# A hybrid attention, state space and dilated attention block on one core: 64-row attention operands without zeros, other queues for the state space transfers, another order of the first loads

## The chip, the cores and the metric

One core of a Trainium2 chip runs the whole program. The time is the device time of one execution in microseconds (us). The engines of the core are PE (TensorE, matmuls), DVE (VectorE), ACT (ScalarE), POOL (GpSimd) and SP (SyncE, which issues most DMAs). Weights come from HBM through SBUF; matmuls write PSUM, which DVE and ACT empty.

## The reference, cut to what matters

Two layers over 256 tokens of width 1024, in fp32. The first has three branches on one projection: MLA (causal attention of 8 heads with 128 channels of nope and 64 of rope), gated linear attention in chunks (GLA) and attention to a memory of 256 tokens (4 heads of 64 channels), gated and summed, and then a feed-forward net (FFN). The second has a state space branch (S5, here as a chunked convolution and a scan over chunks) and dilated attention (3 groups of 8 heads with 64 channels).

```python
q_full = jnp.concatenate([q_nope, q_pe], axis=-1)          # 128 + 64 channels
k_full = jnp.concatenate([k_nope, jnp.broadcast_to(k_pe, (B, S, MLA_HEADS, MLA_ROPE))], axis=-1)
o_mla = causal_block_attention(q_full, k_full, v_mla, (MLA_NOPE + MLA_ROPE) ** -0.5)
...
s_m = jnp.einsum('bshd,bmhd->bhsm', q_m, k_m).astype(jnp.float32) * (MEM_DQK ** -0.5)   # 64 channels
p_m = jax.nn.softmax(s_m, axis=-1).astype(v_m.dtype)
...
bu_re = jnp.einsum('blgp,gnp->blgn', u_c, bb_re)           # the state space: 64 groups, 16 channels, 64 states
y = jnp.einsum('blgn,gpn->blgp', h_re, cr) - jnp.einsum('blgn,gpn->blgp', h_im, ci)
...
s = jnp.einsum('bqhd,bqjhd->bqhj', q_blk[:, :, g], kg) * scale   # dilated: 64 channels a head
```

## The kernel before

The code doesn't call the engines at once. A recorder (L538) writes every operation into a plan, and `Plan.order` (L356) sets the order in which each engine gets its instructions: `Plan.price` (L283) gives each operation a cost, `latest` (L320) works back from the end to due times, and `order` walks forward through time and takes for each engine the ready operation with the earliest due time. `boost` raises some of them, the first loads above all, by `START` (L163). All is emitted at one line (L535), so the rows of the profile all say L535 and are told apart by their tiles: ps is PSUM, wr a weight chunk as loaded, wh and wl its fp32r main part and remainder (written by ACT and DVE), k tiles of activations (their pools k2, k4 and kx are not told apart), c constants, sm small ones. `nc.any` lets the plan choose DVE or ACT.

The large products are in fp32r, three passes (high by high, high by low, low by high), each of 256 or 512 columns. Attention is in fp32, which the profile shows as two records of MATMUL for each instruction. What the parts of the change touch:

- `apart` (L774) writes a transposed operand with two heads, one on rows 0 to 63 and one on 64 to 127, into two tiles that are zero in the other half (GpSimd writes the zeros). With them the scores of one 64-channel head are a matmul over all 128 rows. It serves MLA's rope keys (`kpT`, L937), the memory keys (`kmT`, L891) and the keys of dilated group 0 (`heads`, L1543).
- `mla_attn` (L1154) does for each head the scores of the nope channels and of the rope channels into one PSUM tile (128 columns for the first 128 queries, 256 for the others), then softmax on DVE and ACT, transposes on PE, and the product with the values. `mem_attn` (L1092) and `dilated` (L1578) are alike; `dilated` adds the 64 by 64 blocks of groups 1 and 2 behind each group 0 product.
- `ssm_quarter` (L1367, four times, recorded among the FFN) makes the S5 matrices: PE transposes them, one copy for each half of them goes from PSUM to `gx`, and four SBUF to SBUF DMAs on SP bring its four quarters to `g`, on other partitions. A Toeplitz table is written to DRAM (`kz`, two DMAs a quarter) and `ssm_toeplitz` (L1436) reads it back in 16 pieces T of 16 partitions. `ssm_in` (L1461) sends u to DRAM (`ud`) and reads it back regrouped as U; all on SP's queue, among the weights.
- `inputs1` (L847) and `weights` (L603) set the start: gains, memT and the first w_mv chunks on SP's queue. The first w_mv chunk comes in two halves.

Of the kernel before, what the change touches and what calls it, by code (L numbers as in the profile page):

```python
# [19 lines left out]
P = 128  # L20
S = 256
# [124 lines left out]
PE, ACT, DVE, POOL, SP = "tensor", "scalar", "vector", "gpsimd", "sync"  # L146
# [8 lines left out]
START = {"w_mv": 0, "x": 7.2, "rows": 16, "mem": 20, "w_mk": 40}  # L155
WARM = 10
NORM = 500000
# [10 lines left out]
LAG.update({(ACT, ACT): 145, (PE, PE): 0, (DVE, PE): 220, (ACT, PE): 240})  # L168
READ_FIRST = ("copy_predicated",)
# [6 lines left out]
class Plan:  # L176
# [379 lines left out]
class Net:  # L556
# [46 lines left out]
    def weights(self, name, idx, nk, n):  # L603
# [3 lines left out]
        for i in range(nk // 2):  # L607
# [5 lines left out]
            for k in [slice(0, 1), slice(1, 2)] if name == "w_mv" and idx + i == 0 else [slice(0, 2)]:  # L613
# [160 lines left out]
    def apart(self, z, gain=None):  # L774


        nc = self.nc
        half = slice(0, 64), slice(64, P)
        for i in range(2):
            nc.gpsimd.memset(z[i][half[1 - i]], 0.0)  # L780

        def evac(b, n, p):
            for i in range(2):
                nc.any.copy(z[i][half[i], b:b + n], p[half[i]], *([] if gain is None else [gain[half[i]]]))
        return evac

# [60 lines left out]
    def inputs1(self):  # L847
# [10 lines left out]
        self.gains = self.load_const("gains", [P, GW])  # L858
# [21 lines left out]
    def mem_kv(self):  # L880
# [10 lines left out]
        self.kmT = [self.t2([P, 2, S]) for _ in range(2)]  # L891
        self.transposed(km.rearrange("p t h d -> p t (h d)"), 2, self.apart(self.kmT, self.g("g_k_mem")))
# [21 lines left out]
    def ckv(self):  # L914
# [22 lines left out]
        self.kpT = [self.const([P, 1, S]) for _ in range(2)]  # L937
        self.transposed(kd.rearrange("p t h d -> p t (h d)"), 1, self.apart(self.kpT))
# [153 lines left out]
    def mem_attn(self):  # L1092
# [7 lines left out]
        for hh in range(4):  # L1100
            p = self.aux([P, 512])
# [3 lines left out]
            pr = self.t2([P, 512])  # L1105
            self.softmax_rows(p, pr, [256, 256])
            pT = self.aux([P, 2, S])
# [259 lines left out]
    def ssm_quarter(self, qd):  # L1367
# [58 lines left out]
        k = 1  # L1426
# [400 lines left out]
```

## Time and profile before

| | us |
|---|---|
| median of 3 runs (lowest to highest) | 864.33 (863.37 to 865.55) |
| the profiled execution, its own time | 864.48 |
| its span, first to last instruction | 862.7 |
| busy in the span: PE, DVE, ACT, POOL | 845.5, 630.5, 471.6, 5.4 |
| mean granted clock of TensorE | 0.997 |

Busy time of an engine is the time in which it has at least one instruction. Matmuls are pipelined, and the shown duration of one holds its latency too, so that what a matmul costs is read from the start of one to the start of the next. "PEclk" is the granted clock, 1.00 for 2.4 GHz. Idle time ahead of a row stands in brackets with the operation that ended it. SPq is SP's DMA queue: the time beside it is that of issuing, not of moving the data.

### The profile page before, as it was taken

Reading aid. Unit: us, or ns where it says so; the run is one execution under the profiler, and the core shown is the slowest. Engines: PE = TensorE matmul, PEld = TensorE weight load, DVE = VectorE, ACT = ScalarE, POOL = GpSimd, SP = SyncE. Lnnn points to the kernel's source line nnn. Section 1 sums busy time; section 2 is a strip of 40 time slices with the busy share of each in tenths; the row PEclk is TensorE's granted clock in tenths of the full one; section 3 lists DMA queues with packets and bytes.
Section 4 is the critical chain, followed back from the end, with each engine's and each line's share of the span. In section 5 each row is a group of like instructions: output and inputs, shape, how many; then the busy total and the mean of one; then the engine's idle time right before and its main releaser. Section 6 shows DMA issues by size and latency. Waiting matters only on the chain.

```text
span 862.7 us, 16680 instructions
## 1 busy us (share of the span) xinstructions
PE 845.5 (98%) x6572; PEld 757.2 (88%) x6572; DVE 630.5 (73%) x1484; ACT 471.6 (55%) x754; POOL 5.4 (1%) x13
## 2 busy tenths in 40 slices
PE   8999998999999999999999999899999999999998
PEld 6988877889999989999999888787789769999996
DVE  6999999995766669964445755969997665653584
ACT  6767756645445557555555564446466653554352
POOL 2000000000000000000000000000000000000000
PEclk9999999999999999999999999999999999999999
DMA  8874433035455564555555579670445404555551
GB/s 317 255 243 150 149 125 119 1 120 177 141 176 175 190 237 154 195 195 193 185 186 182 196 170 237 225 219 29 148 146 174 145 25 138 180 172 195 182 178 56
DMA packets 60750, 144.19 MB, mean 167 GB/s; under 512 B 24560, under 2 KB 25712, under 8 KB 60672
## 3 DMA queue, kind: packets, MB, share of 16 engines
q1 hardware_dynamic: 60672, 143.13, 50.7%
q8 instruction: 51, 0.84, 0.4%
q14 instruction: 27, 0.22, 0.1%
HBM read 138.46 MB, written 2.56 MB: 163 GB/s over the span
## 4 chain that ended last, share of the span: by engine, by line
PE 84%; DVE 9%; DMA 2%; ACT 1%; issue 1%; SPq 1%; DVEq 0%; ACTq 0%
PE ps L535 84%; DVE k L535 6%; DVE wl L535 2%; DVE sm L535 1%; SPq L535 1%; ACT k L535 1%; DMA wr<-w_mv 1%; DMA wr<-w_k 1%; ACT wh L535 0%; DMA k<-k 0%; DVE c L535 0%; DVEq L1815 0%; ACTq L535 0%; DVEq L535 0%
## 5 line engine op out<-in xcount | busy, mean ns | idle before, releaser
L535 DVE TENSOR_TENSOR wl<-wr,wh 128x1024 fp32r<-128x1024 f32 (+2 forms) x257 | 300.8, 1193 | 164.0 <-ACT wh L535 161.5
L535 ACT CAST wh<-wr 128x1024 fp32r<-128x1024 f32 (+2 forms) x257 | 257.6, 1028 | 232.7 <-PE ps L535 214.1
L535 PE MATMUL ps<-k,wh 128*128 128x256 f32 x2048 | 371.3, 283 | 0.3 <-DVE k L535 0.3
L535 PEld LDWEIGHTS ps<-k,wh 128*128 128x128 f32 x2048 | 320.2, 192 | 2.0 <-DVE k L535 0.5
L535 PE MATMUL ps<-wh,k 128*128 128x512 f32 (+2 forms) x1024 | 313.8, 384 | 2.3 <-ACT wh L535 2.2
L535 PE MATMUL ps<-k,wl 128*128 128x256 f32 x1024 | 289.9, 283 | 1.9 <-DVE wl L535 1.9
L535 PEld LDWEIGHTS ps<-wh,k 128*128 128x128 f32 x1024 | 188.8, 188 | 38.7 <-ACT wh L535 3.3
L535 PEld LDWEIGHTS ps<-k,wl 128*128 128x128 f32 x1024 | 196.4, 192 | 3.0 <-DVE wl L535 2.3
L535 PE MATMUL ps<-wl,k 128*128 128x512 f32 (+2 forms) x512 | 196.9, 386 | 1.3 <-DVE wl L535 1.2
L535 PEld LDWEIGHTS ps<-wl,k 128*128 128x128 f32 x512 | 96.2, 188 | 21.0 <-DVE wl L535 3.6
L535 DVE TENSOR_TENSOR k<-k,k 128x512 f32<-128x512 f32 (+8 forms) x192 | 91.8, 497 | 13.2 <-ACT k L535 12.7
L535 PE MATMUL ps<-k,k 64*64 64x64 f32 (+6 forms) x1224 | 83.5, 253 | 2.6 <-ACT k L535 1.4
L535 PEld LDWEIGHTS ps<-k,k 64*64 64x64 f32 (+4 forms) x1224 | 62.4, 139 | 21.3 <-issue 12.3
L535 ACT ACTIVATE k<-ps 128x512 f32<-128x512 f32 (+2 forms) x86 | 44.4, 531 | 45.9 <-PE ps L535 45.7
L535 ACT COPY k<-ps 128x512 f32<-128x512 f32 (+7 forms) x98 | 44.1, 491 | 35.0 <-PE ps L535 31.5
L535 ACT ACTIVATE k<-k 128x512 f32<-128x512 f32 (+3 forms) x71 | 45.9, 673 | 24.3 <-DVE k L535 23.4
L535 PE MATMUL ps<-c,k 128*128 128x128 f32 (+1 forms) x344 | 54.3, 286 | 4.2 <-DVE k L535 3.0
L535 PEld LDWEIGHTS ps<-c,k 128*128 128x128 f32 x344 | 41.2, 147 | 11.8 <-DVE k L535 3.9
L535 DVE TENSOR_TENSOR k<-k,c 128x64 f32<-128x64 f32 (+7 forms) x176 | 47.6, 314 | 0.0
L535 ACT ACTIVATE k<-ps,c 128x256 f32<-128x256 f32 (+3 forms) x79 | 38.5, 544 | 14.0 <-PE ps L535 12.0
L535 DVE SCALAR_TENSOR_TENSOR k<-k,k 128x256 fp32r<-128x256 f32 (+4 forms) x61 | 32.6, 567 | 12.3 <-ACT k L535 12.1
L535 ACT ACTIVATE k<-k,sm 128x384 f32<-128x384 f32 (+2 forms) x32 | 16.8, 528 | 10.9 <-DVE sm L535 10.9
(73 smaller groups left out, 302.7 us busy)
## 6 DMA issues: line engine op xcount, KB each, us to landing
wr<-w_up SPq DMA_DIRECT2D x32, 512.0 KB, 3.6
wr<-w_down SPq DMA_DIRECT2D x32, 512.0 KB, 3.6
wr<-w_gt SPq DMA_DIRECT2D x24, 512.0 KB, 4.1
wr<-w_o SPq DMA_DIRECT2D x16, 512.0 KB, 3.8
wr<-w_k SPq DMA_DIRECT2D x12, 512.0 KB, 4.1
wr<-w_q SPq DMA_DIRECT2D x12, 512.0 KB, 4.2
wr<-w_v SPq DMA_DIRECT2D x12, 512.0 KB, 3.3
wr<-w_qkg SPq DMA_DIRECT2D x8, 512.0 KB, 4.3
```

The costliest lines, as they stand in the source:

```text
L535: getattr(getattr(tc.nc, op.eng), op.name)(*map(live, op.args), **{k: live(v) for k, v in op.kw.items()})
```

## The change

- `apart` is gone. Keys with 64 channels stay in one tile, two heads on its two row halves, and the scores of a head are a matmul of 64 rows by 128 columns on its half. In `mla_attn` both heads of a pair get their PSUM tile first; the code writes the nope products of both, and then the rope products in turns between the halves. `mem_attn` goes by pairs too, in turns. `dilated` changes its operands only.
- `price` halves the cost of such a matmul, and a GpSimd DMA is 700 there instead of 1000.
- `gx` and its four DMAs a quarter are gone: eight half-size copies a quarter go from PSUM straight to the right partitions of `g`, where two stood before.
- kz, T, ud and U transfers are issued by GpSimd (`nc.gpsimd`).
- gains is issued by ACT. The first two w_mv chunks come in halves (`HALVES`), and x is due behind more w_mv chunks (12.2 in `START`, 7.2 before).

```diff
-START = {"w_mv": 0, "x": 7.2, "rows": 16, "mem": 20, "w_mk": 40}
+START = {"w_mv": 0, "x": 12.2, "rows": 16, "mem": 20, "w_mk": 40}
+HALVES = 2
...
-            return {SP: 50, ACT: 50, POOL: 1000}[op.eng]
+            return {SP: 50, ACT: 50, POOL: 700}[op.eng]
...
-            if half:
-                return 2 * (2 * n / 2.4 + cols / 1.2 - 8)
-            return 2 * (max(2 * n / 2.4, cols / 1.2) + 9)
+            return (1 if half else 2) * (max(2 * n / 2.4, cols / 1.2) + 9)
...
-            for k in [slice(0, 1), slice(1, 2)] if name == "w_mv" and idx + i == 0 else [slice(0, 2)]:
+            for k in [slice(0, 1), slice(1, 2)] if name == "w_mv" and idx + i < HALVES else [slice(0, 2)]:
...
-        self.gains = self.load_const("gains", [P, GW])
+        self.gains = self.const([P, GW])
+        nc.scalar.dma_start(out=self.gains, in_=I["gains"])
...
-        self.kpT = [self.const([P, 1, S]) for _ in range(2)]
-        self.transposed(kd.rearrange("p t h d -> p t (h d)"), 1, self.apart(self.kpT))
+        self.kpT = self.const([P, 1, S])
+        self.transposed(kd.rearrange("p t h d -> p t (h d)"), 1, lambda b, n, p: nc.any.copy(self.kpT, p))
...
+            ps = [self.aux([P, 512]) for _ in HALF]
             for t in range(2):
-                nc.tensor.matmul(p[:, t * S:(t + 1) * S], qmT[:, hh // 2, t * P:(t + 1) * P],
-                                 self.kmT[hh % 2][:, hh // 2], start=True, stop=True)
+                for i, hs in enumerate(HALF):
+                    nc.tensor.matmul(ps[i][:, t * S:(t + 1) * S], qmT[hs, hp, t * P:(t + 1) * P],
+                                     self.kmT[hs, hp], start=True, stop=True)
...
+            ps = [self.aux([P, 384]) for _ in HALF]
+            for i, p in enumerate(ps):
                 hh = 2 * hp + i
-                kp = self.kpT[i][:, 0]
-                nc.tensor.matmul(p[:, 0:P], qn(0), self.kT[hh][:, 0:P], start=True, stop=False)
-                nc.tensor.matmul(p[:, 0:P], qp(0), kp[:, 0:P], start=False, stop=True)
-                nc.tensor.matmul(p[:, P:384], qn(1), self.kT[hh], start=True, stop=False)
-                nc.tensor.matmul(p[:, P:384], qp(1), kp, start=False, stop=True)
+                nc.tensor.matmul(p[:, 0:P], self.qT[hh][:, 0:P], self.kT[hh][:, 0:P], start=True, stop=False, skip_group_check=True)
+                nc.tensor.matmul(p[:, P:384], self.qT[hh][:, P:], self.kT[hh], start=False, stop=False, skip_group_check=True)
+            for t, ks in enumerate((slice(0, P), slice(P, 384))):
+                for p, hs in zip(ps, HALF):
+                    nc.tensor.matmul(p[:, ks], self.qpT[hs, hp, t * P:(t + 1) * P], self.kpT[hs, 0, 0:P * (t + 1)],
+                                     start=False, stop=True, skip_group_check=True)
...
-        for gh in range(2):
-            for par in range(2):
-                nc.sync.dma_start(out=g[64 * gh:64 * gh + 64, :, par], in_=gx[64 * par:64 * par + 64, :, gh])
+            for gh in range(2):
+                for par in range(2):
+                    nc.any.copy(g[64 * gh:64 * gh + 64, 4 * ri:4 * ri + 4, par], p[64 * par:64 * par + 64, :, 64 * gh:64 * gh + 64])
...
-                    self.nc.sync.dma_start(out=self.T[par][o:o + 16],
+                    self.nc.gpsimd.dma_start(out=self.T[par][o:o + 16],
...
-                nc.sync.dma_start(out=ud[qd].rearrange("(gs q) (e c) -> (q e) gs c", gs=8, e=8),
+                nc.gpsimd.dma_start(out=ud[qd].rearrange("(gs q) (e c) -> (q e) gs c", gs=8, e=8),
...
-                    nc.tensor.matmul(pp[i][:, 0:S], self.q2[0][:, b, tt * P:tt * P + P], self.k2T[0][i][:, b],
+                    nc.tensor.matmul(pp[i][:, 0:S], self.q2[0][a, b, tt * P:tt * P + P], self.k2T[0][a, b],
```

The plan sets a new order for the whole program. First PE, in the MLA attention. Of before, the end of one head (ps_2341) and the next one of the pair (ps_2367): the PSUM tile takes nope products (from k_405) and rope products (c_2 and c_6 are the two zero-padded key tiles, k_399 the rope queries) by turns, all over 128 rows.

```order
L535 MATMUL ps_2341<-c_2_95,k_399_1596 128x256
L535 MATMUL ps_2330<-k_543_2322,k_419_1666 128x128
L535 MATMUL ps_2367<-k_405_1619,k_546_2332 128x128
L535 MATMUL ps_2367<-c_6_105,k_399_1596 128x128
L535 MATMUL ps_2367<-k_405_1619,k_546_2332 128x256
L535 MATMUL ps_2367<-c_6_105,k_399_1596 128x256
```

Of after, the two heads of a pair (ps_2282 and ps_2307): the products from c_383 (rope keys) and k_387 (rope queries) are the 64-row ones, each head's on its own row half.

```order
L535 MATMUL ps_2282<-k_393_1584,k_518_2245 128x128
L535 MATMUL ps_2282<-k_393_1584,k_518_2245 128x256
L535 MATMUL ps_2282<-c_383_1550,k_387_1562 128x128
L535 MATMUL ps_2282<-c_383_1550,k_387_1562 128x256
L535 MATMUL ps_2299<-c_39_232,k_511_2211 128x128 x4
L535 MATMUL ps_2307<-k_393_1584,k_518_2245 128x128
L535 MATMUL ps_2307<-k_393_1584,k_518_2245 128x256
L535 MATMUL ps_2307<-c_383_1550,k_387_1562 128x128
L535 MATMUL ps_2307<-c_383_1550,k_387_1562 128x256
```

The two 64-row products of a head now stand behind its two full-array ones, and between the two heads of the pair stand other full-array matmuls. In the memory attention, after, the same in a closer mix (ps_2448 to ps_2491 are the scores of the four heads, 64 rows each; c_39 is the identity of the transposes):

```order
L535 MATMUL ps_2448<-k_408_1634,k_581_2437 128x256 x2
L535 MATMUL ps_2439<-k_584_2444,k_403_1621 128x256
L535 MATMUL ps_2466<-k_408_1634,k_581_2437 128x256
L535 MATMUL ps_2469<-c_39_232,k_575_2411 128x128
L535 MATMUL ps_2466<-k_408_1634,k_581_2437 128x256
L535 MATMUL ps_2439<-k_584_2444,k_406_1628 128x128
L535 MATMUL ps_2480<-k_408_1634,k_581_2437 128x256
L535 MATMUL ps_2469<-c_39_232,k_575_2411 128x128 x2
L535 MATMUL ps_2480<-k_408_1634,k_581_2437 128x256
L535 MATMUL ps_2491<-k_408_1634,k_581_2437 128x256 x2
```

The heads of ps_2448 and ps_2480 lie on rows 0 to 63, those of ps_2466 and ps_2491 on rows 64 to 127; before, each head's two products stood together, over all rows. Counted over the whole program, PE changes the shape of its tile 120 times before and 156 times after. On DVE, 623 instructions stand ahead of the last of the twelve softmax reciprocals of MLA and memory attention before, and 561 after.

Second the queues of the state space. Before, SP has all of it between the weights (kz writes, the copies to `g` as k<-k, ud, T as k<-kz, U as k<-ud):

```order
L535 DMA k_1308_6434<-k_1295_6342 64x8x64 x4
L535 DMA ud_58<-k_1309_6471 128x8x64
L535 DMA k_1315_6498<-kz 16x16x64 x7
L535 DMA wr_6516<-w_u 128x1024
L535 DMA wr_6524<-w_k 128x1024
L535 DMA k_1315_6498<-kz 16x16x64
L535 DMA k_1319_6535<-kz 16x16x64
L535 DMA k_1320_6539<-ud_58 128x512
L535 DMA k_1319_6535<-kz 16x16x64 x3
L535 DMA wr_6566<-w_k 128x1024
```

After, GpSimd's queue has it, in this order, with nothing else between:

```order
L535 DMA kz<-k_1274_6274 64x2x64 x2
L535 DMA k_1301_6389<-kz 16x16x64 x8
L535 DMA k_1305_6466<-kz 16x16x64 x5
L535 DMA ud_58<-k_1310_6502 128x8x64
L535 DMA k_1305_6466<-kz 16x16x64 x3
L535 DMA k_1314_6546<-ud_58 128x512
L535 DMA ud_59<-k_1310_6502 128x8x64
L535 DMA k_1314_6546<-ud_59 128x512
```

SP keeps only the weights there. On GpSimd sixteen T transfers stand ahead of U's first read, thirteen of them ahead of the write of ud; on SP nine stood ahead of it, all behind that write.

## Rows read from the trace of the kernel before

**Rows 1.** From the page: busy time, share and instructions of each engine, and the chain of work that ended last, its shares by engine.

```profile
PE 845.5 (98%) x6572; PEld 757.2 (88%) x6572; DVE 630.5 (73%) x1484; ACT 471.6 (55%) x754; POOL 5.4 (1%) x13
...
PE 84%; DVE 9%; DMA 2%; ACT 1%; issue 1%; SPq 1%; DVEq 0%; ACTq 0%
```

**Rows 2.** From the timeline of PE around 143 to 151 us (MLA attention): start in us, us to the end of the group, engine, line, operation, output and inputs, rows by columns of the array, shape; x counts records, two for an fp32 matmul.

```profile
143.03 1.82 PE L535 MATMUL ps<-c,k 128*128 128x128 f32 x10 [1.69 <-DVE k L535]
...
148.93 0.38 PE L535 MATMUL ps<-k,k 128*128 128x128 f32 x2
149.99 0.49 PE L535 MATMUL ps<-k,k 128*128 128x128 f32 x2 [0.68 <-ACT k L535]
150.32 0.39 PE L535 MATMUL ps<-c,k 128*128 128x128 f32 x2
150.54 0.60 PE L535 MATMUL ps<-k,k 128*128 128x256 f32 x2
150.97 0.70 PE L535 MATMUL ps<-c,k 128*128 128x256 f32 x3
```

**Rows 3.** From the timeline of PE at the decay gate (the product of 16 rows), columns as in rows 2.

```profile
74.68 0.28 PE L535 MATMUL ps<-k,wl 128*128 128x256 f32 x1
74.80 0.40 PE L535 MATMUL ps<-k,wh 128*128 128x256 f32 x2
75.13 1.12 PE L535 MATMUL ps<-c,k 16*128 16x256 f32 x4
76.19 0.39 PE L535 MATMUL ps<-k,wl 128*128 128x256 f32 x1
76.41 0.27 PE L535 MATMUL ps<-c,k 128*128 128x128 f32 x1
```

**Rows 4.** From the timeline of PE in the dilated attention, columns as in rows 2; the first row holds 15 matmuls of 64 by 64 and two of 128 by 256.

```profile
679.14 2.48 PE L535 MATMUL ps<-k,k 64*64 64x64 f32 x34
681.55 0.50 PE L535 MATMUL ps<-wl,k 128*128 128x512 f32 x1
```

**Rows 5.** From the groups of instructions of PE by line, operation, tile and form over the whole span: records, busy us, mean ns of one, idle before.

```profile
L535 PE MATMUL ps<-k,k 64*64 64x64 f32 x768 | 29.6, 223 | 1.6 <-DMA k<-ud 0.6 <-DVE k L535 0.5 <-ACT k L535 0.4
...
L535 PE MATMUL ps<-k,k 128*64 128x64 f32 x64 | 4.3, 227 | 0.0
```

**Rows 6.** From the windows by stage of the attention region: stretch, its us, busy time (instructions) of PE, PEld, DVE, ACT and POOL, granted clock, DMA share, GB/s.

```profile
126.50:141.00 14.50, 14.50 (x302) 13.07 (x292) 14.11 (x67) 10.35 (x24) 0.00 (x0) 1.00 0.24 78
141.00:150.00 9.00, 6.56 (x63) 5.15 (x52) 7.29 (x21) 4.15 (x11) 0.00 (x0) 0.81 0.62 204
150.00:158.00 8.00, 7.70 (x51) 6.87 (x52) 7.82 (x46) 4.92 (x16) 0.00 (x0) 1.00 0.10 38
166.00:174.00 8.00, 8.00 (x44) 6.73 (x43) 8.00 (x46) 5.33 (x14) 0.00 (x0) 1.00 0.01 3
```

**Rows 7.** From the timeline of SP's DMA queue at the start.

```profile
1.19 0.42 SPq L535 DMA_DIRECT2D c<-gains  x1
1.66 0.42 SPq L535 DMA_DIRECT2D wr<-w_mv  x1
```

**Rows 8.** From the timeline of ACT at the start.

```profile
4.75 0.62 ACT L535 CAST wh<-wr 128x512 fp32r<-128x512 f32 x1 [0.76 <-DMA wr<-w_mv]
...
6.93 0.62 ACT L535 CAST wh<-wr 128x512 fp32r<-128x512 f32 x1 [0.86 <-DMA wr<-w_mv]
8.82 0.91 ACT L535 ACTIVATE k<-k,c 128x256 fp32r<-128x256 f32 x2 [1.28 <-DMA k<-memT]
10.11 1.04 ACT L535 CAST wh<-wr 128x1024 fp32r<-128x1024 f32 x1 [0.37 <-DMA wr<-w_mv]
```

**Rows 9.** From the timeline of SP's DMA queue at the state space transfers, us of issuing and count in each row.

```profile
508.80 5.43 SPq L535 DMA_DIRECT2D k<-k  x8
514.28 1.99 SPq L535 DMA_DIRECT2D kz<-k  x3
...
519.14 0.58 SPq L535 DMA_DIRECT2D ud<-k  x1
519.90 4.65 SPq L535 DMA_DIRECT2D k<-kz  x7
```

**Rows 10.** From the windows of the same stretch, columns as in rows 6.

```profile
500.00:520.00 20.00, 18.93 (x206) 17.70 (x205) 11.08 (x34) 11.64 (x29) 0.00 (x0) 1.00 0.76 168
520.00:545.00 25.00, 22.81 (x171) 19.20 (x170) 14.80 (x23) 10.74 (x13) 0.00 (x0) 1.00 0.93 246
```

**Rows 11.** From the timeline of PE, ACT and DVE from 530 to 546 us (u, and the first products of the state space).

```profile
532.27 0.33 PE L535 MATMUL ps<-k,k 64*64 64x64 f32 x4 [0.64 <-DMA k<-ud]
...
534.88 1.05 ACT L535 CAST wh<-wr 128x1024 fp32r<-128x1024 f32 x1 [3.34 <-DMA wr<-w_k]
...
542.19 1.21 DVE L535 TENSOR_TENSOR_SCAN k<-k,k 128x512 f32<-128x512 f32 x1
...
544.08 1.21 DVE L535 TENSOR_TENSOR wl<-wr,wh 128x1024 fp32r<-128x1024 f32 x1
...
545.34 0.39 PE L535 MATMUL ps<-k,wl 128*128 128x256 f32 x1 [1.89 <-DVE wl L535]
```

**Rows 12.** From the DMA issues by tile: count, KB of each, median us from issue to landing.

```profile
ud<-k SPq DMA_DIRECT2D x4, 256.0 KB, 5.0
...
k<-ud SPq DMA_DIRECT2D x4, 256.0 KB, 4.3
```

More of the change, by code (lines that the diff above doesn't have):

```diff
@@ L168 @@
 LAG.update({(ACT, ACT): 145, (PE, PE): 0, (DVE, PE): 220, (ACT, PE): 240})
+HALF = slice(0, 64), slice(64, P)
 READ_FIRST = ("copy_predicated",)
@@ L772, in split @@
             nc.vector.scalar_tensor_tensor(lo, src, scale, h.bitcast(F32), ALU.mult, ALU.subtract)
[L774 to L785, printed above, removed]
     def row_rms(self, x, n):
@@ L890, in mem_kv @@
         km = self.normed(ps, 0, 4, 64, r)
-        self.kmT = [self.t2([P, 2, S]) for _ in range(2)]
-        self.transposed(km.rearrange("p t h d -> p t (h d)"), 2, self.apart(self.kmT, self.g("g_k_mem")))
+        self.kmT = self.t2([P, 2, S])
+        self.transposed(km.rearrange("p t h d -> p t (h d)"), 2,
+                        lambda b, n, p: nc.any.copy(self.kmT[:, b:b + n], p, self.g("g_k_mem")))
     def norm_x(self):
@@ L1157, in mla_attn @@
             o = self.aux([P, 2, S])
[L1158 removed]
+            ps = [self.aux([P, 384]) for _ in HALF]
+            for i, p in enumerate(ps):
                 hh = 2 * hp + i
[L1160 to L1167 removed]
+                nc.tensor.matmul(p[:, 0:P], self.qT[hh][:, 0:P], self.kT[hh][:, 0:P], start=True, stop=False, skip_group_check=True)
[4 more added lines that the diff above has]
+                                     start=False, stop=True, skip_group_check=True)
+            for i, p in enumerate(ps):
+                hh = 2 * hp + i
                 pr = self.t2([P, 384])
@@ L1349, in ssm_small @@
         nc.vector.memset(z, 0.0)
-        nc.sync.dma_start(out=self.kz.rearrange("g a j q x -> (g a j q) x")[:, 0:48].rearrange("(p r) x -> p r x", r=8), in_=z)
+        nc.gpsimd.dma_start(out=self.kz.rearrange("g a j q x -> (g a j q) x")[:, 0:48].rearrange("(p r) x -> p r x", r=8), in_=z)
         self.G, self.Cx, self.R = [], [], []
@@ L1548, in heads @@
             self.rope(q[:, :, :, 0:16], 8, ta, tb, 8, q[:, :, :, 0:16])
-            if g == 0 and nm == "kr":
-                qt = [self.t4([P, 4, S]) for _ in range(2)]
-                evac = self.apart(qt, self.g(gain, g))
-            else:
-                qt = self.t4([P, 4, S])
-                evac = lambda b, n, p: self.nc.any.copy(qt[:, b:b + n], p, self.g(gain, g))
-            self.transposed(q.rearrange("p t h d -> p t (h d)"), 4, evac)
+            qt = self.t4([P, 4, S])
+            self.transposed(q.rearrange("p t h d -> p t (h d)"), 4,
+                            lambda b, n, p: self.nc.any.copy(qt[:, b:b + n], p, self.g(gain, g)))
             dst.append(qt)
@@ L1589, in dilated @@
                 pp = [self.aux([P, 384]) for _ in half]
-                for i in range(2):
-                    nc.tensor.matmul(pp[i][:, 0:S], self.q2[0][:, b, tt * P:tt * P + P], self.k2T[0][i][:, b],
+                for i, a in enumerate(half):
+                    nc.tensor.matmul(pp[i][:, 0:S], self.q2[0][a, b, tt * P:tt * P + P], self.k2T[0][a, b],
                                      start=True, stop=False, skip_group_check=True)
```

41 lines of the change are left out of this document (18 added, 23 removed).

## The prediction

> **What bounds the kernel now.** I read the page first. TensorE (PE) is busy for 98% of the span and the chain that ended last is 84% PE, with 9% DVE [rows 1]. So the time is the sum of PE's issue times, plus the places where PE waits for someone, and an edit counts only if it shortens the first or takes away one of the second. The reader should therefore look for two things in the rest: what a 64-row matmul costs on PE, and where PE stands still.
>
> For the first I read PE's timeline at two places and the groups of PE by form. At 150 us the full-array fp32 matmul (two records, one for each pass) takes 0.22 us for 128 columns of output and 0.43 us for 256, from start to start [rows 2]. The kernel before has one matmul that uses few rows and all 128 columns, the 16-row one of the decay gate: two of them take 1.06 us (75.13 to 76.19) between fp32r matmuls [rows 3]. That is 0.53 each, not less than the full array's 0.43. The fp32r matmul behind them starts its successor after 0.22 us, where its neighbours take 0.12, and the two ahead take 0.33 in place of 0.24. So the excursion into another tile shape and back costs (1.06 - 0.86) + 0.10 + 0.09 = 0.39 us, about 0.195 for each of two switches, and fewer rows by themselves buy nothing. A second place bounds it from below: 15 matmuls of 64 by 64 and two of 128 by 256 lie between 679.14 and 681.55 [rows 4]. By 0.058 each (they alternate between row halves; the whole group's busy time gives 29.6/384 = 0.077, [rows 5]) and 0.43 each they would need 0.87 + 0.86 = 1.73 of the 2.41 us, which leaves 0.68 for five switches, 0.14 each.
>
> For the second I read the windows by stage. From 126 to 184 us DVE is nearly always busy; between 141 and 150 PE is busy for only 6.56 of 9 us and its granted clock is 0.81 [rows 6]; the half-speed level (1.2 GHz) lies right behind PE's longest idle stretch there, 1.69 us ahead of 143.03, which ended with DVE [rows 2].
>
> **The change part by part.**
>
> *Unpadded halves.* Forty matmuls (16 of the MLA rope scores, 8 of the memory attention, 16 of the dilated group 0) lose their 64 rows of zeros. By rows 3 each keeps its length when it stands alone. It would be cheaper if two of them ran side by side on the two row halves: the 64 by 64 ones do so, at 0.077 us where the 128-row 64-column form takes 4.3/32 = 0.134 [rows 5]. But the emitted order decides, and it puts the halves of an MLA pair each with its own head: two full-array matmuls, two on one half, two full-array ones of the other head, two on the other half. In the memory attention only one pair of neighbours changes halves with nothing between (worth about 0.2 us, not counted); in the dilated part each stands ahead of its own four 64 by 64. So the planner's order undoes the turns that the code writes, and what is left is the switches. In the built order PE changes its tile shape 120 times before and 156 times after: 24 more in the MLA and memory attention (8 MLA blocks and 5 memory blocks, 26 switches, 2 of which fall where a switch stood already), 12 net in the rest. The first are of the kind of rows 3, 24 x 0.195 = 4.7 us; for the others I take the lower 0.14, 1.7 us. Sum **+6.4 us**, bounds 36 x 0.14 = 5.0 and 36 x 0.195 = 7.0. All of it is on PE, which covers nothing. The lower bound falls further if two shapes on the same 64 rows (64 by 128 next to 64 by 64, 22 such switches in after) need no switch at all: then it is 7.0 - 22 x 0.195 = 2.7. No row shows that pair. The evacuations that wrote the padded copies in two halves go away too, on ACT and DVE; off the path.
>
> *What the new order does in the attention region.* Ahead of the twelfth and last softmax reciprocal DVE has 623 instructions in the order before and 561 after. At 46 in 8.00 us (166 to 174, [rows 6]) the 62 fewer are worth 10.8 us of DVE, and PE comes there some 4 us later by the switches. PE waits for DVE there by little at a time, so a lead of this size should end the waits. They are worth, between 141 and 158: 2.44 + 0.30 us of PE not busy, and (1 - 0.81) x 9 = 1.7 us of half clock that follows the idle stretch [rows 6]: **-4.5 us**. Bounds: 0, if the same tail of scans and copies ends last whatever stands behind it; 6, since modelled ends hide a part of each wait: from 148.93 to 149.99 one matmul of 0.22 us takes 1.06, where the row shows 0.68 of idle [rows 2].
>
> *First loads.* gains leaves SP's queue for ACT's, so w_mv's first half is issued one step earlier, 1.19 in place of 1.66, and all behind it [rows 7]. ACT's casts at 4.75 and 6.93 waited for their w_mv, the one at 10.11 too, and that last one is 1.04 us long because its chunk comes in one piece [rows 8]; halved it lets PE start after 0.62. x goes behind later w_mv chunks and so gives those its place. 0.47 + 0.42 = **-0.9 us**, bounds 0 (if memT ends last, which ACT waited 1.28 for at 8.82) and -1.5. ACT's own DMA issue stands ahead of its table load and costs it some 0.4 us; its cover is ACT's idle time ahead of 4.75, of which 0.76 us is a wait for w_mv [rows 8].
>
> *State space transfers.* Sixteen SBUF to SBUF copies go (eight of them took 5.43 us of SP's queue, [rows 9]); in their place 32 evacuations of half size stand where there were 8. A cast of 1024 columns is 1.05 us on ACT [rows 11], so one of 256 columns is under 0.5, and all 32 are under 16 us, spread over the FFN. From 500 to 545 ACT is busy for 22.4 and DVE for 25.9 of 45 us [rows 10], so idle time covers them; without that cover at most a few tenths of each quarter's copies would reach PE. The kz, T and ud transfers go from SP to GpSimd's queue. That frees SP for weights: T and U0's read stand from 519.90 among the w_k and w_u issues, U0 landed so that PE waited 0.64 us at 532.27, ACT waited 3.34 us for w_k at 534.88, and PE waited 1.89 at 545.34 for a wl that stood behind DVE's scan batch [rows 9, 11]. In the new DVE order that wl follows the scans at about the time PE needs it. 0.6 + 1.4 = **-2.0 us**, bounds -3 and +0 (GpSimd's own cost is a rival).
>
> Sum, against the profiled execution's 864.48: 864.48 + 6.4 - 4.5 - 0.9 - 2.0 = **863.5 us**. That execution is 0.15 us over the median of the runs (864.33), far less than any term.
>
> **The rivals.**
>
> *GpSimd is late.* Nothing of before issues a DMA from GpSimd, so its price has only far bounds: SP's T issue takes 4.65/7 = 0.66 us [rows 9]. In after thirteen T transfers and then ud0's write stand on GpSimd ahead of U0's read (three more T within the write's landing time), and PE comes to U0 94 matmuls after u's last one, some 16 us by their durations (13 in before: ud0's write at 519.14, U0 used at 532.27). kz's last writes, at 514.28, stood behind 5.43 us of copies on SP, so they could leave at about 509 and land by 512. With 5.0 + 4.3 us for ud's write and read [rows 12] and PE at U0 at about 535, an issue may take (535 - 512 - 9.3)/14 = 1.0 us; each 0.1 above costs 1.4 us. If a GpSimd issue has to fit into DVE's gaps (DVE busy for 25.9 of 45 us, 58%), 0.66/0.42 = 1.57, so PE waits 8 us at U0: 871.5; at 1.2 it is 866. The Trainium skill, SBUF — State Buffer, the box on the "DVE blocks DMA" trap, states such a rule: GpSimd writes its descriptors through a port that DVE's two-port copies lock. No run here shows it yet, and it speaks against this change.
>
> *The halves do run in turns.* If the array takes a 64-row matmul on the other half while the first still runs, though other work stands between, or if the shapes on the same rows need no switch: half of 8 x 0.22 + 32 x 0.43 = 15.5 us is 7.8, so 863.5 - 7.8 = 855.7; with the switches of the same rows alone free, 863.5 - 3.7 = 859.8. For it: the 64 by 64 groups cost half. Against it: the order, and the length of the 16-row matmul in rows 3. The Trainium skill, TensorEngine Tiling (Array Packing), Theoretical Speedup, gives up to 2 for a small dimension of 64; by that the time would be the 855.7.
>
> *The waits only move.* DVE's lead is not there, or PE meets ACT in DVE's place: nothing of the 4.5 and half of the 2.0 comes, 863.5 + 5.5 = 869.0. It decides from a lead of less than 4 us.
>
> *The waits go further.* A DVE with 10 us less ahead also smooths 161 to 200 us and SP's relief the later FFN and q, k, v gemms: another 2 to 4 us, 860.5.
>
> **How the numbers follow.** Chances: forecast 0.38, GpSimd late 0.17, halves in turns or free switches 0.23, waits only move 0.12, waits go further 0.10. The forecast's own range is 860.5 to 867.5, its bounds not all at once. What a measurement can tell here is 0.3%, 2.6 us: 861.7 to 866.9 counts as the same. Faster: 0.23 + 0.10 + 0.08 of the forecast = 0.41. Slower: 0.12 + 0.13 + 0.03 = 0.28, with 0.04 of the late GpSimd mild enough for the same. Same: 0.31. The range leaves out the far half of the turns below and the far ends of GpSimd and of the moved waits above: 857 to 870.
>
> **What would show it.** Right: in PE's timeline of after the fp32 scores of 128 by 256 stay at 0.43 us with 0.09 to 0.1 more on each side of a 64-row block; between 134 and 165 us PE's busy share is full and its clock 1.00; PE's waits for wh and DVE before 14 us shrink by about one; no wait for ud, and less than 1 us for wl near 545. Wrong: 64-row pairs that end within 0.5 us of each other, or a wait of PE for k from ud of more than a microsecond, or the half clock again at 145.

## The result and the profile after

| | before | after |
|---|---|---|
| median of the runs beside each other, us | 864.94 | 874.86 |
| ratio to before, 95% interval | | 1.0119 (1.0081 to 1.0157) |
| profiled span, us | 862.7 | 872.8 |
| changes of PE's tile shape in the built order | 120 | 156 |
| sum of PE's issue times, us | 835.2 | 842.6 |

The change made the kernel 10 us slower; 863.5 was predicted. The sum of issue times takes for each matmul its time from start to start as rows 2 and 3 show it (0.43 for fp32 of 256 columns, 0.12 for fp32r of 256, half for a matmul that is followed by one on another tile of the same shape, 0.1 at each side of a change of shape). What PE took beyond that sum in a stretch is called its loss below. Over the program the sum rose by 7.4 us and the loss by 2.5.

The page of after, with busy times and chain [rows 1]:

```profile
PE 853.1 (98%) x6572; PEld 757.7 (87%) x6572; DVE 631.4 (72%) x1478; ACT 477.4 (55%) x782; POOL 22.6 (3%) x40
...
PE 86%; DVE 7%; ACT 3%; issue 2%; DMA 1%; SPq 0%; DVEq 0%; POOL 0%; ACTq 0%; POOLq 0%
```

The page looks like before; the windows of after don't, columns as in rows 6 [rows 6, 10]:

```profile
95.00:106.00 11.00, 8.20 (x48) 6.36 (x46) 11.00 (x16) 7.87 (x12) 0.00 (x0) 1.00 0.50 143
...
141.00:150.00 9.00, 9.00 (x59) 6.83 (x58) 6.59 (x28) 8.27 (x19) 0.00 (x0) 1.00 0.41 117
...
500.00:520.00 20.00, 16.30 (x179) 14.67 (x169) 11.37 (x37) 17.97 (x48) 12.16 (x21) 0.91 0.44 111
520.00:545.00 25.00, 25.00 (x196) 22.04 (x196) 14.95 (x23) 9.94 (x14) 4.07 (x6) 1.00 0.67 208
...
580.00:600.00 20.00, 16.43 (x244) 14.10 (x242) 13.34 (x32) 9.50 (x16) 0.56 (x1) 0.91 0.46 155
```

Between 141 and 150 us PE no longer stands still and its clock is full. It stands still in three other places: 2.8 us between 95 and 106, 3.7 between 500 and 520, and 3.6 between 580 and 600, the latter two with a clock of 0.91. The start of PE's n-th matmul in both traces tells where the 10 us were lost:

| n-th matmul of PE | 400 | 1200 | 3200 | 3300 | 3600 | 3800 | 4200 | 4600 | 5700 |
|---|---|---|---|---|---|---|---|---|---|
| before, us | 76.9 | 202.9 | 498.5 | 506.4 | 556.6 | 586.6 | 642.6 | 711.7 | 849.4 |
| after, us | 75.0 | 203.3 | 498.9 | 510.3 | 558.1 | 593.5 | 650.5 | 721.6 | 859.4 |
| difference | -1.9 | +0.4 | +0.4 | +3.9 | +1.5 | +6.9 | +7.9 | +9.9 | +10.0 |

The whole first layer, with its new switches, costs 0.4 us. The border of the layers costs 3.5, the state space part gives 2.4 back and then costs 5.4, and what follows, the dilated attention above all, some 3. There PE changes its tile shape 68 times instead of 53, which at 0.195 us each is 2.9 of it.

At the border, the timeline of DVE, ACT and PE in after:

```profile
504.89 1.90 ACT L535 COPY k<-ps 64x256 f32<-64x256 f32 x5
...
506.83 0.43 DVE L535 COPY k<-ps 64x256 f32<-64x256 f32 x1 [1.56 <-ACT k L535]
507.29 0.16 DVE L535 SCALAR_TENSOR_TENSOR sm<-sm,sm 128x2 f32<-128x2 f32 x1
...
507.48 0.42 DVE L535 COPY k<-ps 64x256 f32<-64x256 f32 x1
507.93 0.16 DVE L535 SCALAR_TENSOR_TENSOR sm<-sm,sm 128x2 f32<-128x2 f32 x1
508.12 1.42 DVE L535 TENSOR_SCALAR k<-k,sm 128x1024 f32<-128x1024 f32 x2
...
509.02 0.83 PE L535 MATMUL ps<-c,k 128*128 128x128 f32 x3 [3.22 <-DVE k L535]
```

The reader sees two of the new half-size evacuations (64x256) on DVE between the last steps of the second layer's norm (the 128x2 operations on sm, then the scaling of the tokens), the first of them held 1.56 us by ACT, which works through the other copies. PE waits 3.22 us for the scaled tokens.

In the second half of the state space part, ACT and PE of after:

```profile
587.43 1.05 ACT L535 CAST wh<-wr 128x1024 fp32r<-128x1024 f32 x1 [0.33 <-PE ps L535]
588.38 0.68 ACT L535 ACTIVATE k<-ps,c 128x512 f32<-128x512 f32 x1
589.81 1.08 ACT L535 ACTIVATE k<-ps 128x512 f32<-128x512 f32 x2 [0.75 <-PE ps L535]
```

```profile
589.12 0.66 PE L535 MATMUL ps<-c,k 128*128 128x128 f32 x4 [1.29 <-ACT k L535]
591.52 5.28 PE L535 MATMUL ps<-k,k 64*64 64x64 f32 x128 [1.75 <-ACT k L535]
```

PE has come to transposes whose source ACT writes last, with no weight product left in between as filler; the order of before has such products there.

GpSimd's issues were not the bound. Its queue in after:

```profile
509.20 7.26 POOL L535 DMA_DIRECT2D k<-kz  x13 [2.48 <-DMA kz<-k]
523.08 0.91 POOL L535 DMA_DIRECT2D ud<-k  x1 [6.61 <-ACT k L535]
```

A T transfer takes 7.26/13 = 0.56 us to issue, less than SP's 0.66 [rows 9], with DVE busy for 3.57 us of the 7.30 from 509.20 on. The queue then waits for u, which ACT writes, and later for ud's data.

### The profile page after: what moved, and what is told of

Same layout as the page of the kernel before. It is cut to its first block, busy times and chain, and to the rows that moved or that the text cites. A ratio compares the mean times of both kernels' runs of the same rounds, so it can differ in the third digit from the quotient of the medians.

```text
span 872.8 us, 16700 instructions
## 1 busy us (share of the span) xinstructions
PE 853.1 (98%) x6572; PEld 757.7 (87%) x6572; DVE 631.4 (72%) x1478; ACT 477.4 (55%) x782; POOL 22.6 (3%) x40
## 4 chain that ended last, share of the span: by engine, by line
PE 86%; DVE 7%; ACT 3%; issue 2%; DMA 1%; SPq 0%; DVEq 0%; POOL 0%; ACTq 0%; POOLq 0%
PE ps L535 86%; DVE k L535 5%; ACT k L535 2%; DVE sm L535 1%; DVE wl L535 1%; ACT wh L535 1%; DMA wr<-w_mv 1%; DMA k<-ud 1%; SPq L535 0%; DVE c L535 0%; ACT L535 0%; ACT c L535 0%; DVEq L1804 0%; POOL ud L535 0%; ACTq L535 0%
## 5 line engine op out<-in xcount | busy, mean ns | idle before, releaser
L535 PE MATMUL ps<-k,k 64*64 64x64 f32 (+7 forms) x1224 | 85.7, 256 | 2.7 <-ACT k L535 2.2
L535 PEld LDWEIGHTS ps<-k,k 64*64 64x64 f32 (+5 forms) x1224 | 62.3, 142 | 23.7 <-issue 13.5
L535 ACT COPY k<-ps 128x512 f32<-128x512 f32 (+7 forms) x119 | 50.7, 456 | 35.1 <-PE ps L535 34.1
L535 PE MATMUL ps<-c,k 128*128 128x128 f32 (+3 forms) x344 | 57.0, 296 | 7.2 <-DVE k L535 3.9
L535 PEld LDWEIGHTS ps<-c,k 128*128 128x128 f32 (+2 forms) x344 | 40.8, 149 | 19.6 <-ACT k L535 7.1
L535 ACT ACTIVATE k<-ps,c 128x256 f32<-128x256 f32 (+2 forms) x76 | 37.0, 540 | 16.3 <-PE ps L535 16.3
L535 DVE CUSTOM_DVE_ANT_0 k<-ps,c 128x384 f32<-128x384 f32 (+2 forms) x32 | 14.4, 455 | 10.3 <-PE ps L535 10.2
```

The lines of the kernel that those rows point to most:

```text
L535: getattr(getattr(tc.nc, op.eng), op.name)(*map(live, op.args), **{k: live(v) for k, v in op.kw.items()})
```

## The experiments

Of every run the median is given, then the ratio to before on the same chip with its interval. The losses are read from each trace by the rule above.

**Each part alone on the kernel before.**

```diff
 e1  START x 12.2, HALVES = 2, gains by nc.scalar.dma_start
 e2  kz, T, ud, U by nc.gpsimd.dma_start; POOL: 700
 e3  gx and its DMAs replaced by the eight copies a quarter
 e4  64-row operands (MLA, memory, dilated) and the halved price
```

> The kernel before with the first loads alone changed (gains issued by ACT, two w_mv chunks in halves, x later). By the theory that the start is worth what it showed in the changed kernel (PE's loss ahead of 28 us fell from 7.0 to 6.0 us) and that the new waits of PE at 97 and 104 us come from DVE and ACT being asked for w_mv's halves and x in a new order, this one is 1.0 us faster at the start and loses up to 2.8 us again by 113 us: 863 to 866. By the rival that those waits come only from the whole new order, it is 863.3 and shows no wait of PE over 1 us between 90 and 113 us but the 1.1 us of the kernel before.

861.89, 0.9955 (0.9938 to 0.9973): faster, and under what either side gave. PE's loss ahead of 25 us is 5.3 (6.1 before), and no new wait stands at 97 us; so the waits there in the changed kernel are not the loads'. The start explains 0.8 of the 3.0 us. The rest is the new order elsewhere: between 125 and 200 us the loss is some 4.4 us less than before, between 515 and 560 some 2 us more.

> The kernel before with kz, T, ud and U issued by GpSimd, and the plan's price for that, alone. By the theory that GpSimd's transfers make U late (ud to U took 5.4 + 3.9 us plus queueing in the changed kernel, and PE stood still for 4.8 us in all between 573 and 594), it is 3 to 5 us slower, 867 to 869, with PE waiting for k from ud or for ACT there. By the rival that the queue is harmless (a T issue took 0.56 us of GpSimd) and the loss came from the order, it is 862.5 to 864.5, with the wait for wl at 545 (1.9 us) gone or halved.

864.25, 0.9988 (0.9972 to 1.0003): no difference, as the rival said.

> The kernel before with the sixteen SBUF to SBUF copies replaced by 32 half-size evacuations alone. By the theory that these stand on DVE and ACT ahead of the second layer's norm (in the changed kernel four of 0.43 us on DVE, one behind 1.56 us of waiting for ACT, held the norm's last steps, and PE waited 3.4 us at 505.5 where it had lost 0.9), it is 2 to 3 us slower: 866.5 to 867.5, with that wait at 505. By the rival that they find room when the rest of the order stays, it is 863.5 to 865.

865.94, 1.0013 (0.9997 to 1.0029), between the two. The wait at the border is there as the theory said: PE waits 3.7 us between 480 and 515, and 1.1 before. By releaser (us in total, times, longest), e3:

```profile
PE ps L535 <- DVE k L535: 2.8, 2, 2.4
PE ps L535 <- ACT k L535: 0.9, 1, 0.9
```

and before:

```profile
PE ps L535 <- ACT k L535: 0.8, 1, 0.8
PE ps L535 <- DVE k L535: 0.3, 1, 0.3
```

But the time is the same within the noise, since the stretch from 515 to 560 loses 2.8 us less.

> The kernel before with the unpadded halves and their price alone. In its order PE changes tile shape 129 times (before 120, changed kernel 156), so by the switch price of 0.19 us its issue times grow by 1.9 us. By the theory that switches are the only effect on PE it is 866.2, less what of the 5.8 us of waits at 141 to 161 us goes away: 861 to 866. By the rival that the halves run side by side it would be 7 us faster, 857.

864.85, 1.0003 (0.9982 to 1.0024). Issue times +1.9, loss between 125 and 200 us 0.4 instead of 6.3, loss between 60 and 125 us 5.8 instead of 1.9, so the new waits there come with the halves. The halves don't run side by side, since in this order too none stands next to one of the other half.

The parts alone add up to -0.4%, together they give +1.2%. No price of a part explains that.

**Parts together.** These four were to be the changed kernel less one part each, and the expectations speak of that; but the kernels that ran kept more of before, and have the old matmul price and padded MLA and memory keys throughout. f1 is before with GpSimd transfers and the dilated halves, f2 with loads, evacuations and dilated halves, f3 with loads, GpSimd transfers and dilated halves, f4 with loads and GpSimd transfers. Their shape changes and issue times are as stated, but the rivals' times belong to kernels that did not run.

> The changed kernel with the old first loads. The theory after the first four runs (alone, the parts cost -0.45, -0.1, +0.1 and 0.0%, together +1.2%): no part has a price of its own that adds up; the plan's order of the whole decides, through the number of tile shape changes and the places of DVE's and ACT's work. In this one's order PE changes shape 105 times (changed kernel 156, before 120) and PE's issue times sum to 831.8 us by the durations seen so far (842.6 and 835.2). With the 29 to 32 us of waits, start and end of the two kernels: 861 to 864. Rival, parts with fixed prices: the changed kernel's 874.9 and the 3 us that the loads alone gave, 878.

856.13, 0.9877 (0.9856 to 0.9898): 5 us under the theory's range.

> The changed kernel with the state space transfers on SP and their old price. By the theory of the order: 101 shape changes, issue times of 831.0 us, 860 to 863. By the rival of fixed prices (the GpSimd queue alone gave -0.1%, U late in the changed kernel took 4.8 us): 870 to 876.

854.09, 0.9863 (0.9846 to 0.9881): 6 us under the theory's range. The wait at the border is there (3.7 us), as in each kernel with evacuations.

> The changed kernel with the SBUF to SBUF copies by DMA, as before. By the theory of the order: 99 shape changes, issue times of 830.5 us, 859.5 to 862.5; the wait ahead of the second layer's norm (3.4 us at 505.5) is gone, since no evacuation stands in DVE's chain there. By the rival of fixed prices: 874.9 less 1 to 3 us, 872 to 874.

855.10, 0.9873 (0.9857 to 0.9888): 4 us under the theory's range. PE waits 0.9 us at the border.

> The changed kernel with zero-padded keys and the old matmul prices. By the theory of the order: 103 shape changes, issue times of 831.7 us, 860.5 to 864. By the rival that the 64-row matmuls' own switches are the 7.5 us of issue time in the changed kernel, and the rest of its loss stays: 867.

861.71, 0.9946 (0.9928 to 0.9965): inside the theory's range, and just what e1 and e2 alone add up to (0.9943).

So three different mixtures of the same parts are 1.2 to 1.4% faster, by their issue times of 830.5 to 831.8 us and by losses of 16.5 to 19.9 us (22.9 before); the theory had put in the losses of the two first kernels, and so was too high. In all three the state space part has 13 to 15 shape changes where before has 36, the changed kernel 32, and f4 some 25.

What the three share, and f4 lacks, is the dilated group 0 with 64-row operands. All seven kernels with padded dilated keys (before, e1, e2, e3, f4 and, below, h1 and p2) have 21 to 36 shape changes in the state space part; of the twelve with 64-row ones, ten have 13 to 15, and only the changed kernel and t1 have 32. No run has this operand alone on the kernel before. So that part may draw the better order, and the changed kernel and t1 may be the exceptions; it is not shown.

**The plan's luck by itself.** A transpose's price in the plan is raised by 1 ns; the operations are the same ones.

```diff
-            return 110
+            return 111
```

> The changed kernel with one number of the plan's prices changed, 111 ns instead of 110 for a transpose; the operations are the same ones. The order that comes out has 133 shape changes instead of 156 (15 instead of 32 in the state space part) and issue times of 838.0 us instead of 842.6. By the theory that the order's luck in the state space part is a term of its own: 864 to 871. By the rival that the change costs what it costs in any order: 873 to 876.

The changed kernel: 865.99, 1.0004 (0.9983 to 1.0025), inside what the theory gave: 8.9 us less than the changed kernel.

> The kernel before with 111 ns for a transpose in the plan's prices instead of 110, nothing else. 101 shape changes instead of 120 (19 instead of 36 in the state space part), issue times 831.4 us instead of 835.2. By the theory that the order's luck is a term of its own for any kernel of this plan: 858 to 862, clearly faster than before. By the rival that only the changed kernel's order is that sensitive: 863.5 to 866.

The kernel before: 860.63, 0.9944 (0.9923 to 0.9966), clearly faster, as the theory said. So 1 ns in a price, which changes no operation, moves these kernels by 4 to 9 us; the change's 10 us is of that size.

**What a half and a change of shape cost.** Extra matmuls on zeros ahead of the first product:

```diff
+        for _ in range(4):
+            part(pa, A)
+            part(pb, B)
+        for _ in range(4):
+            full(pc)
+            part(pa, A)
...
+        for _ in range(4):
+            part(pa, A)
+            part(pa, A, 64, A)
```

> The kernel before with 80 extra fp32 matmuls on zeros ahead of its first product (they feed nothing), each of 128 columns by 256 unless told otherwise: 8 of 128 rows; 8 of 64 rows on one half; 8 of 64 rows in turns between the halves; 128 and 64 rows by turns (8); groups of 2 full, 2 on one half, 2 full, 2 on the other half (as the changed kernel's MLA, 16); groups of 4 full and 4 in turns (16); 64 by 128 and 64 by 64 on the same rows by turns (8); 8 of 128 rows. By the prices that I worked out: full 0.43 each, one half 0.43 each, in turns 0.22, 0.195 for each change of shape (so 8 x 0.62, then 16 x 0.43 + 8 x 0.195 = 8.4, then 16 matmuls 8 x 0.43 + 8 x 0.22 + 4 x 0.195 = 6.0), and 0.195 for the change from 64 by 128 to 64 by 64. Rivals: a half alone takes half the time; the halves do not overlap; the change on the same rows is free.

The windows of this run, one for each group (stretch, its us, PE busy with records; two for each matmul, and one or more of the neighbours):

```profile
5.49:9.14 3.65, 3.65 (x17) 2.96 (x16) 1.68 (x4) 1.73 (x4) 0.69 (x1) 1.00 0.95 304
9.14:12.48 3.34, 3.34 (x17) 2.94 (x18) 2.41 (x5) 2.87 (x5) 0.00 (x0) 1.00 1.03 417
12.48:14.52 2.04, 2.04 (x19) 1.59 (x16) 2.04 (x5) 1.55 (x3) 0.00 (x0) 1.00 1.03 404
14.52:19.54 5.02, 5.02 (x18) 2.37 (x17) 2.23 (x6) 2.54 (x5) 0.00 (x0) 1.00 1.04 410
19.54:28.01 8.47, 8.47 (x34) 5.38 (x33) 7.85 (x58) 4.63 (x13) 0.00 (x0) 1.00 0.92 286
28.01:33.89 5.88, 5.88 (x34) 4.44 (x33) 5.88 (x65) 0.95 (x6) 0.00 (x0) 1.00 0.00 0
33.89:37.31 3.42, 3.42 (x19) 1.83 (x16) 3.42 (x45) 0.00 (x0) 0.00 (x0) 1.00 0.01 2
```

From start to start: full 0.432, one half alone 0.432, in turns 0.216 (the third window, where the last one takes 0.52, with no other half beside it and a change of shape behind), full and half by turns 0.627 each, so 0.195 for a change of shape. Sixteen in the changed kernel's MLA order take 8.47 us, sixteen with four in turns 5.88. On the same rows 64 by 128 and 64 by 64 take 0.626 and 0.255 by turns. With 0.06 to 0.13 for a 64 by 64 matmul without a change of shape (the prediction's 0.058 and 0.134), that change costs as well, 0.16 to 0.20 each. All this is one execution. The prices were as worked out; the rivals fall.

**Halves that really stand in turns.** The plan gets dependencies and a boost for the 64-row matmuls:

```diff
+    def chain(self, after, boost=200000):
+        op = self.plan.ops[-1]
+        op.deps |= set(after)
+        if boost:
+            op.boost = boost
+        return [op.i]
...
+                    last = self.chain(last)
```

> The changed kernel, with dependencies and a boost in the plan that make the 64-row matmuls of a pair really stand in turns (25 of the 40 next to one of the other half; the changed kernel has one such place). Tile shape changes 117 instead of 156, issue times 829.9 us instead of 842.6. By the theory that halves in turns cost half and a change of shape 0.195 us: 12.7 us less than the changed kernel, 860 to 864. By the rival that the halves do not overlap, 4.5 us more than that: 865 to 868. By the rival that the loss of the changed kernel is its DMA queue and its evacuations: 872.

861.53, 0.9945 (0.9929 to 0.9960): 13.3 us under the changed kernel, as the theory said, with its waits at the border and around 590 still there.

> The changed kernel with the turns of the run before last, and the old price of 1000 ns for a GpSimd DMA in the plan: 90 shape changes, 13 of them in the state space part (32 in the changed kernel, 36 before), issue times 824.1 us. By the theory of shape changes and turns: 824.1 and the 29 us of waits, start and end that the good orders so far had around them, 849 to 854, faster than both kernels. By the rival that halves don't overlap: 854 to 858.

848.13, 0.9789 (0.9772 to 0.9807): under the range of the theory (849 to 854) by 1 us, faster than both kernels. It has the operations of t1, and one price of the plan is another. That alone is 13.4 us, the largest step of this kind here: 27 fewer shape changes, and a loss of some 0.8 us between 560 and 600 where t1 has some 6.6.

The groups of PE by form show the halves themselves (records, busy us, mean ns). In the changed kernel:

```profile
L535 PE MATMUL ps<-k,k 64*128 64x256 f32 x48 | 15.5, 424 | 0.0
L535 PE MATMUL ps<-c,k 64*128 64x256 f32 x16 | 4.8, 377 | 0.0
L535 PE MATMUL ps<-c,k 64*128 64x128 f32 x16 | 3.9, 322 | 0.0
```

and in the fastest run below, t7:

```profile
L535 PE MATMUL ps<-k,k 64*128 64x256 f32 x48 | 7.9, 420 | 0.0
L535 PE MATMUL ps<-c,k 64*128 64x256 f32 x16 | 2.4, 377 | 0.0
L535 PE MATMUL ps<-c,k 64*128 64x128 f32 x16 | 2.0, 323 | 0.0
```

PE shows one of these 40 matmuls at work for 24.2 us in the one and 12.3 in the other. From the start of each to the start of the next matmul they take 20.8 and 10.6 us, a change of shape behind them included. The record of a single one is as long in both.

**What is left of the other parts once the halves stand in turns.**

> The changed kernel with padded keys and the old matmul prices, all else as changed (the kernel that was meant by f4_no_halves). 114 shape changes, 25 in the first layer's attention instead of 50, 30 in the state space part; issue times 834.2 us. By the theory that the halves out of turns are the main loss: 8.4 us of issue time less than the changed kernel, 864 to 868. By the rival of a single bad order that goes with everything: 872 to 876.

The changed kernel with padded keys (no turns): 873.79, 1.0090 (1.0066 to 1.0115). My theory fell here, the rival's 872 to 876 holds. Its issue times are 8.4 us less, its loss 33.9 us instead of 25.4: 6.4 us between 125 and 200 us are back (0.2 in the changed kernel), and 4.6 between 25 and 60 are new. The waits between 125 and 200 us go with DVE's order and not with the switches. In DVE's order of h1, 633 instructions stand ahead of the last softmax reciprocal (623 before, 561 in the changed kernel). The six kernels with 623 or more (before, e2, e3, f4, h1, p2) lose 4 to 6.4 us there, and the thirteen with 621 or fewer under 2, padded keys or not. So the padded keys saved 8.4 us of issue time, and the order that came with them lost as much again.

> The changed kernel with the halves forced into turns and the sixteen SBUF to SBUF copies by DMA, as before. 94 shape changes, issue times 825.2 us (824.1 in the fastest run so far). By the theory that the evacuations hold the second layer's norm in every order (PE's waits there are 2.8 to 3.5 us in all six kernels with evacuations and 0.6 to 1.1 in the six without, and the clock falls behind them, 0.83 to 0.91 over 20 us): 3 to 5 us less than that fastest run's 848.1, 842 to 846.5. By the rival that the wait is the order's luck: 847 to 851.

846.23, 0.9779 (0.9759 to 0.9799), at the upper end of the theory's range. At the border PE waits 0.8 us (0.8 to 1.4 in all kernels without evacuations). But PE then waits 2.4 us ahead of a product with U at 570.86 ("issue" in the row, as GpSimd's transfer of U runs), so the total is 1.9 us less, not 3 to 5.

> The changed kernel with the halves forced into turns and the state space transfers on SP, evacuations kept. 92 shape changes, issue times 824.6 us. By the theory that the queue of these transfers is worth nothing by itself (alone it gave -0.1%): 847 to 851, with the wait at 505 of about 3 us and no long wait for U. By the rival that GpSimd's queue costs time in the changed kernel: 844 or less; by the rival that it gains (SP free for weights): over 852.

847.07, 0.9790 (0.9771 to 0.9809): the border's wait (3.7 us) is there, that for U is not. No gain and no loss by the queue: 1.1 us under t3, with intervals that overlap.

> The kernel before with the unpadded halves forced into turns and the new first loads; the copies by DMA and all transfers on SP, as before. 92 shape changes, issue times 824.5 us. By the theory that the evacuations and the GpSimd queue each cost a wait (2.4 us ahead of the second norm and the clock behind it; 2.4 us for U in the run without evacuations) and gain nothing: 842 to 845.5, under the 846.2 of the run with GpSimd and the 847.1 of the run with evacuations. By the rival that SP's queue is then the next to be late, as in the kernel before (PE waited 0.6 us for U and 1.9 for wl): 846 to 850.

844.90, 0.9759 (0.9733 to 0.9786): the fastest kernel of all, with neither the evacuations nor GpSimd's transfers. PE's waits in it, by releaser:

```profile
PE ps L535 <- DVE wl L535: 3.0, 5, 0.9
PE ps L535 <- DVE k L535: 2.6, 5, 1.0
PE ps L535 <- ACT wh L535: 2.1, 3, 1.6
PE ps L535 <- DMA k<-ud: 1.4, 1, 1.4
```

No single wait is over 1.6 us; U is late by 1.4 on SP's queue too.

> The kernel before with the unpadded halves forced into turns alone, old first loads. The same issue times as the run beside it, 824.5 us. By the theory that the start is worth 1 to 3 us whatever the order: 1 to 3 us over the run beside it, 844 to 848. By the rival that the first loads' gain of 0.45% was the order's: the same as the run beside it within 1 us.

846.24, 0.9772 (0.9749 to 0.9794): 1.3 us over t7, with intervals that overlap.

## Why the prediction was wrong, point by point

The prediction added up to -1.0 us, and +10.0 came. By the table above the first layer stands 1.1 us over the terms for it (+0.4 for -0.7), the border and the stretch behind it 3.1 (+1.1 for -2.0), the second half of the state space part 5.4 (nothing was given for it), and the rest 1.4 (+3.1 for the 1.7 of the other switches).

- **A 64-row matmul and its switches: right, a little low.** 6.4 us were given, bounds 5.0 and 7.0; 7.4 came, above the upper one. The lower price of 0.14 for a part of the switches was too low (0.16 to 0.20 in m1_price). That the emitted order undoes the turns was right. The rival of halves in turns fell as it stood: with other work between them two halves don't overlap. Forced next to each other they cost half, as it said (t1_turns).
- **The attention region: right in its place.** PE's loss between 125 and 200 us fell from 6.3 to 0.2 us, 6.1 where 4.5 was given, and the runs bear out that DVE's order decides there; how large a lead it takes is not shown. What had no term is 2.4 us more between 60 and 125 us. All nine kernels with 64-row MLA keys lose some 3 to 6 us there, the ten with padded ones some 2. PE's extra issue time and the waits cancel: +0.4 us at the end of the first layer, where my terms gave about -0.7.
- **First loads: right**, 1.1 us instead of 0.9 (loss ahead of 25 us, 6.1 to 5.0). All twelve kernels with the new loads lose less there than any of the seven with the old ones.
- **State space transfers: this step failed.** It gave -2.0, and +1.1 came there. Its gain came: between 515 and 560 us the loss fell from 3.8 to 1.0. The sentence that idle time of ACT and DVE covers the 32 evacuations was wrong. I took a share of busy time over 45 us for a cover, while the copies stand in DVE's program order between the last steps of the second norm, for which PE waits. In all eight kernels with evacuations PE waited 3.1 to 3.7 us there (changed kernel, e3, f2, h1, t1, t3, t6, p1); in the eleven without, 0.8 to 1.4. The pairs before and e3, and t6 and t7, differ in the evacuations alone, t3 and t5 in one price besides. In time the evacuations cost 1 to 2 us in these pairs, none of them clear of the noise by itself.
- **The rest of the new order was put at nothing, and this failed too.** It is the larger miss. The second half of the state space part lost 5.6 us between 560 and 600 (before 1.3), where the prediction had neither a term nor a rival. The same operations under other prices lose less there: the changed kernel 5.6 and p1 some 2.5, t1 some 6.6 and t3 0.8. So the order decides it, and a changed price in the plan moved whole kernels by 4 to 13 us. The range allowed for 6.5 us on either side of 863.5; one draw of this plan is about as wide by itself. The 15 more shape changes of the dilated part are not such a miss: they belong to the switches, and the prediction had counted them.
- **GpSimd late: not by its issues.** A T took 0.56 us where 1.0 was the limit, PE waited 0.4 us for U. The Trainium skill's rule in SBUF — State Buffer, the box on the "DVE blocks DMA" trap, is not tested by this: during the T issues DVE ran almost only operations that read PSUM, and the box speaks of its two-port copies. In f1, p1 and t5 U came 2.3 to 2.7 us late in other orders (on SP's queue up to 2.0, in e1); by what is not shown.

Every sign of being right that I looked at was there: no half clock at 145, PE full from 134 to 165, 0.6 us for wl near 545, 1.3 us less of waits before 14 us. They were all at places where the kernel before had shown a wait, and the time was lost at others.

Open is whether two parts of the change are worse together. The five kernels with evacuations and GpSimd transfers (changed kernel, h1, p1, t1, t3) lose some 10 to 16 us between 480 and 600, the other fourteen 5 to 8, e1 alone 11. No run has these two parts alone on the kernel before; with the halves in turns, where the order is a good one, the two cost 3.2 us (t3 against t7, on different chips, with intervals that overlap). Open is also why the plan falls into the order with 30 and more shape changes in the state space part: it did in the changed kernel, h1 and t1, but also in before, e1, e2 and e3.

## What to carry to other kernels

Two 64-row matmuls overlap only if they stand next to each other when they are issued, and a change of tile shape costs 0.2 us; so group them in the emitted order by force, and count neighbours there, not in the code. An engine's idle share covers a copy only if the copy doesn't stand in the chain that ends last: look up what stands behind it in its engine's order. Where a planner orders the program, rerun both kernels with a meaningless change of a price before a difference of one per cent is put down to an edit.

## What the runs showed of the hardware that was not expected

PE's clock fell behind the border's wait in some kernels and not in others. Its mean over 500 to 520 us was 0.91 in the changed kernel, 0.86 in h1 and 0.83 in t1, t3 and p1, where one wait of 2.8 to 3.2 us stands there. It was 1.00 in e3, f2 and t6, where 3.7 us came as one wait of 2.4 and one of 0.9. The length of the wait alone doesn't decide it: the half speed behind 143 us in the kernel before followed a wait of 1.69 us [rows 2]. In p1 the clock was 0.66 over 680 to 700 us with PE busy throughout:

```profile
640.00:720.00 80.00, 79.89 (x537) 60.19 (x536) 48.98 (x110) 45.08 (x89) 0.00 (x0) 0.91 0.37 116
...
680.00:700.00 20.00, 20.00 (x115) 12.91 (x112) 11.69 (x35) 9.04 (x22) 0.00 (x0) 0.66 0.12 38
```

These rows are of p1's profiled execution, which took 873.45 us, 7.5 over the median of its runs. At 0.66 of the clock 20 us hold 6.8 us less of full-speed time, so in this execution the half-speed stretch accounts for most of the 7.5 us.
